# Three pieces of order in a two-layer conv and pooling trunk: reloads of x behind their units, and the products and sums of the second modulation column group

## The chip, the cores and the metric

The kernel runs on one core of one Trainium2 chip. The metric is device time in microseconds (us), the median of three runs of the same program; lower is better. A fourth execution was taken by the hardware profiler, and every time inside the kernel below is from that one.

The core's engines work side by side. PE is TensorE, which multiplies matrices; PEld is its load of weights. DVE (VectorE), ACT (ScalarE) and POOL (GpSimd) work on tiles of 128 partitions. SP (SyncE) issues DMAs, and POOL issues some too. In the trace q1 holds the DMAs that SP issues and q0 those that POOL issues.

## The reference

Sequence S = 1024, width D = 1024, feed-forward width F = 2816, two layers, all in fp32. Cut to what matters:

```
c_act = silu(c)
for i in range(2):
    mod = c_act @ ada_w[i] + ada_b[i]
    sh_m, sc_m, g_m, sh_f, sc_f, g_f = split(mod, 6)
    h = rms_norm(x) * (1 + sc_m) + sh_m
    if i == 0: y = conformer_conv(h)     # D->2D, GLU, causal taps of width 31, LayerNorm, silu, D->D
    else:      y = multiscale_pool(h)    # trailing means over 2, 4, 8, 16 minus the token, per-group linear map
    x = x + (1 + g_m) * y
    h = rms_norm(x) * (1 + sc_f) + sh_f
    x = x + (1 + g_f) * ((silu(h @ w_gate) * (h @ w_up)) @ w_down)
return rms_norm(x)
```

The six parts of `mod` are numbered j = 0 to 5 in the kernel; j = 2 is the gate of the mixer, j = 3 the shift of the feed-forward.

## The kernel before

**Products.** The tokens are two chunks, A and B, of 512. A product in fp32 is made of three products of a faster type: each operand is split into a high part and the low remainder, and high by high, high by low and low by high are added up in PSUM (`products`, L485). Most of PE's work is cut into units of 24 matmuls of 128x512 (8 slices of 128, or two halves of 4, by three products). A unit's weight comes as a raw block of 512 KB on SP's queue (tile `raw`); ACT casts it to the high part and DVE makes the low part (tiles `w`). For some weights ACT writes the negated high part, and POOL issues an adding DMA that fetches the weight a second time to make the low part.

**What sets the order.** PE's order is written out by hand: the program is a list of units, and each unit's matmuls stand where they are written. While it is written, a build-time clock adds up what PE, DVE, POOL and ACT should have spent (`clock`). After every 12 or 24 matmuls `pace` (L220) lets the waiting tasks go on: a task is a Python generator that issues its DVE, ACT and POOL instructions, and at times matmuls, in small steps. When a task yields a name, it rests: a name in `LOAD` (L55) lets it rest so many us on PE's clock, a name in `DELAY` (L66) so long behind the DVE and ACT clocks. A task marked `free` may step at every `pace`. `finish(...)` drives tasks to their end on the spot. The order on the other engines is set by a scheduler at build time; an edge (`add_manual_dep(..., edge, ...)`) tells it that an instruction stands behind another in its order, and no semaphore comes of it. Each queue then runs in that order: an SP instruction that waits holds all behind it.

**The modulation columns.** For layer 0, `ada_columns((2, 3))` (L426) computes two of the parts as columns. For each of the 8 slices of D it takes a weight block `adaw` (512 KB, SP's queue, two buffers), and four small matmuls of 32x256 add to a PSUM bank `ada`: one group of products. It yields "load" (4.0 us) ahead of each group, and when a group is done it issues the load two groups ahead. After the eighth group `columns_done` (L449) copies the bank on ACT, yields "spread" (3.0), then two small matmuls (`adac`) turn rows to columns and DVE and POOL write `mod` and the gates. It does this inside the same task, unless j is 3 and `held` is set; then it is put off to `conv_out`. In the program of before that case doesn't come up.

**The conv units and the taps.** `conv_in(*[(A, p) ...], None, *[(B, p) ...])` (L1580) writes the conv's first products for p = 6 and 7 of both chunks; at `None` it finishes the task `norm_b` that makes chunk B's `h`. Two units belong to each p: `a` and `g`. In the rows below `a_1206` is the first unit of chunk B. Behind further units of B come the taps of p = 6 and 7, on PE (`tap`). ACT adds a bias to x by `biased` (L555), which reads `gate_b`, an outcome of column group j = 2.

**The joint phase.** After the first feed-forward units of each layer, `all_joint` (L1649) runs the remaining gate and up products of both chunks jointly, in 11 joint units fp = 0 to 10 of five units of 24 matmuls each, with fewer products by combining operands and by laying partial sums aside (`rd`): the operands n and t are combinations of h, the weights s and others are combinations of four raw quarters (L1010, and by adding DMAs at L1090 and L1078). What a joint unit yields goes through tiles `r`, `t` and `g`; `g` is written to DRAM (`gd<-g`, POOL, L161) for the down products later. The tile `g` rotates, so a new `g` waits until an earlier one has been stored.

**x in DRAM.** Chunk x is spilled to DRAM ahead of this phase (`x_out`, L328: `xd<-x`) and fetched back by `x_in` (L333: `x<-xd`), four blocks of 512 KB a chunk. For chunk A the program calls `x_in(A, fp - 1)` after each of the joint units fp = 1 to 4:

```
for fp in range(NP):
    joint(l, fp)
    if 0 < fp <= KT // 2:
        unit(lambda take, m=fp - 1: x_in(A, m))
```

Nothing ties these four DMAs to PE's order. x is read again by the down products behind the joint phase (from 833 us in layer 0).

Of the kernel before, what the change touches and what calls it, by code (L numbers as in the profile page):

```python
# [19 lines left out]
KT = D // P  # L20
# [31 lines left out]

PE_TAPS = {6: 15, 7: CW}
DIAGS = 8
LOAD = {"load": 4.0, "slow": 6.0, "next": 4.0, "dots": 4.0}  # L55

ON_DVE = (1, 4)
AHEAD = 4
# [69 lines left out]
def trunk(ctx, tc, xT, c, vec, ada, adan, w1f, w1, wdg, w2, wgu, wdn, wpl, out):  # L128
# [8 lines left out]
    last_mm = [None]  # L137
    behind = [False]
    edge = mybir.DependencyInfo(mybir.DependencyClass.NoSync, mybir.DependencyReason.DATA)

    def matmul(out, lhsT, rhs, start, stop, more=False):
        n = out.shape[-1]
        clock["PE"] += n / 2400 * (1 if rhs.dtype == F32R else 4) + 0.0025
        last_mm[0] = nc.tensor.matmul(out, lhsT, rhs, start=start, stop=stop, skip_group_check=more).ins.name  # L144
# [11 lines left out]
    sync = Dma()  # L156
# [47 lines left out]
    def step(t, e):  # L204
        behind[0] = not t.urgent
        before = {k: engines[k].spent for k in "VG"}
        with tc.high_priority(offset=0 if t.urgent else -LATER):
            moved = t.step(e)
        behind[0] = False
        if V_.spent > before["V"] and getattr(t, "dots", False):  # L210
            recent.append(V_.last.ins)
            del recent[:-RECENT]
        if V_.spent > before["V"] and isinstance(t, Taps) and t.ch.i:
            beside.append(V_.last.ins)
            del beside[:-BESIDE]
        for k in "VG":
            clock[k] += (stretch[0] - 1) * (engines[k].spent - before[k])
        return moved
# [13 lines left out]
    def finish(*these):  # L232
        forced[0] = True
        for t in these:
            while not t.done:
                e = "V" if clock["V"] <= clock["G"] else "G"
                o = "VG"[e == "V"]
                if not any(step(q, e) for q in [t] + tasks) and not any(step(q, o) for q in [t] + tasks):
                    raise RuntimeError("nothing moves")
                clock["PE"] = max(clock["PE"], min(clock["V"], clock["G"]))  # L240
        forced[0] = False

    class Task:
# [6 lines left out]
        def step(self, e):  # L250
            if e != "V" or self.done or clock["PE"] < self.until and not forced[0]:
                return False
            try:
# [3 lines left out]
                if said == "wait":  # L257
                    return False
                if said in LOAD:
                    self.until = clock["PE"] + LOAD[said]  # L260
                elif said == "root":
# [12 lines left out]
    def block(tag, name, dt=F32R):  # L274

        pool, bufs = (raws, RAW_BUFS if tag == "raw" else ADA_BUFS) if tag in ("raw", "ada") else (slots, KT if tag[0] == "h" else KT // 2)
        return pool.tile([P, 2, 512], dt, tag=tag, name=nm(name), bufs=bufs)
# [15 lines left out]
    def bank(name):  # L293
        return ps.tile([P, 512], F32, tag="mm", name=nm(name))
# [27 lines left out]
    xp = [[block(f"x{ch.i}", "x", F32) for k in range(KT // 2)] for ch in chunks]  # L322
    x = [[pairs[k // 2][:, k % 2] for k in range(KT)] for pairs in xp]
    xd = [dram.tile([KT // 2, P, 2, 512], F32, name=f"xd_{i}") for i in range(2)]
# [8 lines left out]
    def x_in(ch, only=None):  # L333
        for m in range(KT // 2) if only is None else [only]:
            xp[ch.i][m] = block(f"x{ch.i}", "x", F32)
            sync.dma_start(xp[ch.i][m], xd[ch.i][m])
        x[ch.i][:] = [xp[ch.i][k // 2][:, k % 2] for k in range(KT)]
    for k in range(KT // 2):
        load_next(xp[0][k], xT[0, :, 2 * k : 2 * k + 2])
# [35 lines left out]
    def ada_load(src, queue=sync):  # L375
        w = raws.tile([P, D], F32, tag="ada", name=nm("adaw"), bufs=ADA_BUFS)
        queue.dma_start(w, src)
        return w
# [47 lines left out]
    def ada_columns(js):  # L426


        todo = [(j, k) for j in js for k in range(KT)]
        src = lambda j, k: adan[k, :, (j - 2) * D : (j - 1) * D]  # L430
        ws = [ada_load(src(*t)) for t in todo[:ADA_BUFS]]
        for i, (j, k) in enumerate(todo):
            yield "load"
            if k == 0:
                acc = bank("ada")
            w = ws.pop(0)
            for g in range(4):
                matmul(acc[32 * g : 32 * g + 32, :Q], ccols[:, k, :], w[:, g * Q : g * Q + Q], start=k == 0, stop=k == KT - 1)
            clock["PE"] -= 1.3
            if i + ADA_BUFS < len(todo):  # L440
                ws.append(ada_load(src(*todo[i + ADA_BUFS])))
            if k == KT - 1 and (j != 3 or not held[0]):
                yield from columns_done(j, acc)
            elif k == KT - 1:
                held_back.append((j, acc))

    held, held_back = [False], []

    def columns_done(j, acc):  # L449

        rows = temp(Q)
        S_.copy(rows, acc[:, :Q])
        yield "spread"
        cols = bank("adac")
        for h in range(2):
            matmul(cols[:, 4 * h : 4 * h + 4], rows[:, h * P : h * P + P], quarters, start=True, stop=True)
        m = mod[:, j * KT : (j + 1) * KT]
        V_.tensor_tensor(m.rearrange("p (q h) -> p q h", h=2), cols[:, :KT].rearrange("p (h q) -> p q h", h=2),
                         V("ada_b", j * KT, KT).rearrange("p (q h) -> p q h", h=2), op=ADD)
        ada_gains(0, j, 0, KT, G_)  # L460
        ada_done.add((0, j))
# [150 lines left out]
    def now(gen):  # L612

        while True:
            try:
                next(gen)
            except StopIteration as e:
                return e.value
# [29 lines left out]
    def unit(emit, *weights):  # L648
        units.append((weights, emit))
# [63 lines left out]
    def conv_in(*todo, fine=4):  # L713

        def emit(take):
            got = {}
            for each in todo:
                if each is None:
                    finish(T["norm_b"])
                    continue  # L720
                ch, p = each
                conv_u(ch, p)
                wts = got.setdefault(p, [])
                b = [bank("a"), bank("g")]
                for i in range(2):
                    if len(wts) == i:
                        wts.append(take())
                    for k in range(KT):
                        products(b[i], wts[i], k, st["h", ch.i][k], k == 0, k == KT - 1)
                        if k % fine == fine - 1:  # L730
                            pace()
                conv_glu(ch, p, *b, fine < 4)
                if ch.i == 0 and PE_TAPS.get(p, 0) < CW:
                    T["taps", 0, p] = Taps(A, p)
                if ch.i == 0 and p == KT - 1:
                    for q in PE_TAPS:
                        if PE_TAPS[q] < CW:
                            split_u(q)
        tiles = list(dict.fromkeys(e[1] for e in todo if e))
        unit(emit, *[w1[p, i] for p in tiles for i in range(2)])  # L740

    def split_u(p):

        u = st["u", 0, p][:, HALO - 2 : HALO - 2 + A.n]
        hi, lo = st["us", p] = pair("h0", "us")
        S_.copy(hi, u)
        either(A.n).tensor_tensor(lo, u, hi.bitcast(F32), op=SUB)
# [164 lines left out]
    def conv_out(ch, squares, then=None):  # L912

        def done(d, b):
            update(ch, d, b, gate_m, 0)
            squares.add(d)

        def emit_of(ds):
            def emit(take):
                wts = [take() for _ in ds]  # L920
                bs = [bank("y") for _ in ds]
                for k in range(KT):
                    for wt, b in zip(wts, bs):
                        products(b, wt, k, st["v", ch.i][k], k == 0, k == KT - 1)
                    if len(ds) > 1:
                        pace()
                for d, b in zip(ds, bs):
                    done(d, b)
            return emit
        for ds in [(0, 1) if ch.i else (0,), *(() if ch.i else ((1,),)), *((d,) for d in range(2, KT))]:  # L930
            unit(emit_of(ds), *[direct(w2[d]) if ch.i and d > 1 else w2[d] for d in ds])
            if then is not None and ds[0] == 0:
                unit(then)
# [530 lines left out]
    for k in range(KT):  # L1464
# [4 lines left out]
        if k > 1:  # L1469
            acc = squares[0]  # L1470
# [21 lines left out]
    for k in range(KT + 1):  # L1492
        if k < KT:
            if k:
# [4 lines left out]
                dots = [V_.last.ins]  # L1499
# [34 lines left out]
    T = {}  # L1534
# [50 lines left out]
    for p in PE_TAPS:  # L1585
        for u in pe_taps(p):
            unit(*u)
    unit(lambda take: held.__setitem__(0, True))
    unit(lambda take: finish(T["ada", 0]))
    unit(lambda take: finish(*(T["taps", 0, p] for p in range(KT) if PE_TAPS.get(p, 0) < CW)))  # L1590

    def ada_second(take):
# [7 lines left out]
    unit(lambda take: biased(A))  # L1600
    need("ln_a")
    sq_a = Squares(A, True)
    conv_out(A, sq_a, lambda take: [now(columns_done(*g)) for g in held_back])
    def scale_done(take):
        forced[0] = True
        while (0, 4) not in ada_done:
# [174 lines left out]
```

## Time and profile before

| | |
|---|---|
| three runs | 1740.39, 1738.1, 1740.81 us; median 1740.39 us |
| the profiled execution | 1738.56 us, span 1736.8 us |
| mean granted PE clock | 0.996 of full speed |
| busy, share of the span | PE 98%, DVE 75%, ACT 45%, POOL 27% |
| layer 0: modulation columns, conv units, taps | about 60 to 210 us |
| layer 0: joint phase | about 523 to 834 us |
| layer 1: start of its joint phase | about 1200 us |

In the views of the trace a row of the timeline gives start, duration, engine, line, operation, output and inputs with a count, and in brackets how long the engine had been idle before it and what ended that wait. A row of the chain of waits gives start, duration and what was running, or waited for, on the path that ended last. A row of a table of windows gives, for a stretch of time, its length, the busy time of PE, PEld, DVE, ACT and POOL with the number of instructions, then the granted PE clock, the share of the DMA engines' time that was busy, and GB/s. A DMA's time to landing is from issue to the last byte.

### The profile page before, as it was taken

The numbers are of one execution on the slowest core, as the hardware profiler recorded it, in microseconds if no ns is written. First come the engines' busy times: TensorE is split into PE (matmuls) and PEld (weight loads), VectorE is DVE, ScalarE is ACT, GpSimd is POOL, SyncE is SP. The second block draws the span as 40 slices with busy tenths as digits, with TensorE's granted clock in tenths as the row PEclk, the third lists the DMA queues.
The fourth block names the chain that finished last, engine by engine and source line by source line (L and its number), as shares of the span: only waits on it lengthen the run. The fifth ranks groups of instructions, "written<-read, shape, count | busy, mean of one in ns | idle before, by whom it ended". The sixth has DMA issues, their size and how long they took to land.

```text
span 1736.8 us, 21673 instructions
## 1 busy us (share of the span) xinstructions
PE 1701.5 (98%) x7746; PEld 1386.7 (80%) x7746; DVE 1301.8 (75%) x1878; ACT 788.3 (45%) x1080; POOL 464.2 (27%) x547
## 2 busy tenths in 40 slices
PE   7999999999998999999999999999999999999997
PEld 5777777778886888888888888888788888888887
DVE  8899898899658787887665987848677666555655
ACT  3668686876545233333223347457333333222213
POOL 2588777794001121221110301111111111000001
PEclk9999999999999999999999999999999999999999
DMA  7958987736776888887886837887777574656461
GB/s 291 300 159 236 231 232 193 209 110 198 250 227 182 269 277 244 285 247 254 312 274 214 268 113 223 241 291 202 247 219 219 167 220 141 259 206 207 166 239 56
DMA packets 111453, 385.44 MB, mean 222 GB/s; under 512 B 12145, under 2 KB 14321, under 8 KB 111346
## 3 DMA queue, kind: packets, MB, share of 16 engines
q1 hardware_dynamic: 74832, 256.11, 41.4%
q0 software_dynamic: 35424, 126.89, 29.5%
q8 instruction: 61, 1.00, 0.2%
q10 hardware_dynamic: 1090, 1.05, 0.2%
q14 instruction: 46, 0.38, 0.1%
HBM read 315.85 MB, written 63.96 MB: 219 GB/s over the span
## 4 chain that ended last, share of the span: by engine, by line
PE 87%; DVE 5%; DMA 3%; issue 3%; POOL 1%; ACT 1%; SPq 0%; DVEq 0%; POOLq 0%; ACTq 0%
PE dn L144 26%; PE a L144 22%; PE e L144 12%; PE p L144 11%; PE y L144 6%; PE g L144 3%; PE first L144 3%; PE tap L144 2%; DMA raw<-in_wgu_dram 2%; POOL pa L122 1%; PE ada L144 1%; DMA adaw<-in_adan_dram 1%; PE rstd L144 1%; DVE t L122 1%; DVE w L122 1%
## 5 line engine op out<-in xcount | busy, mean ns | idle before, releaser
L122 ACT CAST w<-raw 128x1024 fp32r<-128x1024 f32 x269 | 281.8, 1050 | 499.4 <-PE dn L144 222.6
L144 PE MATMUL dn<-g,w 128*128 128x512 f32 (+1 forms) x2184 | 484.7, 383 | 1.7 <-DVE g L122 1.0
L144 PEld LDWEIGHTS dn<-g,w 128*128 128x128 f32 x2184 | 399.7, 188 | 82.2 <-DVE g L122 1.3
L122 DVE TENSOR_TENSOR w<-raw,w 128x1024 fp32r<-128x1024 f32 x197 | 244.3, 1243 | 72.8 <-ACT w L122 71.5
L144 PE MATMUL a<-n,w 128*128 128x512 f32 x1056 | 248.0, 390 | 1.1 <-DVE n L122 0.7
L144 PE MATMUL p<-h,w 128*128 128x512 f32 x1056 | 244.1, 390 | 0.9 <-DVE h L122 0.7
L122 POOL TENSOR_TENSOR pa<-pa,pr 128x512 f32<-128x512 f32 x160 | 228.9, 1510 | 22.8 <-ACT pr L122 19.8
L144 PEld LDWEIGHTS a<-n,w 128*128 128x128 f32 x1056 | 197.7, 188 | 44.8 <-DVE n L122 2.2
L144 PEld LDWEIGHTS p<-h,w 128*128 128x128 f32 x1056 | 197.3, 188 | 43.8 <-DVE h L122 1.5
L122 DVE SCALAR_TENSOR_TENSOR x<-dn,gains,x 128x512 f32<-128x512 f32 (+1 forms) x200 | 138.5, 725 | 95.2 <-PE dn L144 95.1
L122 DVE SCALAR_TENSOR_TENSOR ca<-u,vecs,ca 128x512 f32<-128x512 f32 x245 | 169.9, 746 | 0.5
L144 PE MATMUL a<-t,w 128*128 128x512 f32 x528 | 126.5, 395 | 5.7 <-DVE w L122 2.9
L144 PE MATMUL e<-b,w 128*128 128x512 f32 x528 | 123.7, 390 | 1.6 <-DVE t L122 1.0
L144 PE MATMUL e<-t,w 128*128 128x512 f32 x528 | 123.2, 389 | 0.0
L144 PEld LDWEIGHTS a<-t,w 128*128 128x128 f32 x528 | 100.4, 191 | 28.5 <-DVE w L122 4.2
L122 ACT ACTIVATE pr<-u,vecs 128x512 f32<-128x512 f32 x160 | 108.0, 716 | 26.5 <-POOL pa L122 19.8
L144 PEld LDWEIGHTS e<-b,w 128*128 128x128 f32 x528 | 98.9, 188 | 22.9 <-DVE t L122 1.4
L1090 POOL DMA_DIRECT2D raw<-in_wgu_dram x43 | 38.1, 886 | 292.9 <-DMA raw<-in_wgu_dram 129.0
L144 PEld LDWEIGHTS e<-t,w 128*128 128x128 f32 x528 | 99.1, 188 | 20.6
L161 POOL DMA_DIRECT2D gd<-g x76 | 46.9, 619 | 192.5 <-DVE g L122 188.7
L144 PE MATMUL y<-v,w 128*128 128x512 f32 x384 | 89.2, 391 | 0.5 <-DVE v L122 0.5
L144 PEld LDWEIGHTS y<-v,w 128*128 128x128 f32 x384 | 71.5, 188 | 17.5 <-issue 1.6
(164 smaller groups left out, 1971.4 us busy)
## 6 DMA issues: line engine op xcount, KB each, us to landing
raw<-in_wgu_dram SPq DMA_DIRECT2D x132, 512.0 KB, 4.9
raw<-in_wdn_dram SPq DMA_DIRECT2D x88, 512.0 KB, 7.2
gd<-g POOLq DMA_DIRECT2D x76, 512.0 KB, 7.1
g<-gd SPq DMA_DIRECT2D x76, 512.0 KB, 5.9
adaw<-in_ada_dram POOLq DMA_DIRECT2D x48, 512.0 KB, 7.1
raw<-in_wgu_dram POOLq DMA_DIRECT2D x43, 512.0 KB, 7.1
raw<-in_w_dram SPq DMA_DIRECT2D x36, 512.0 KB, 6.6
adaw<-in_adan_dram SPq DMA_DIRECT2D x32, 512.0 KB, 5.5
```

The costliest lines, as they stand in the source:

```text
L122: self.last = self.order(getattr(self.eng, name)(out, *args, **kw))
L144: last_mm[0] = nc.tensor.matmul(out, lhsT, rhs, start=start, stop=stop, skip_group_check=more).ins.name
L161: return order(nc.gpsimd.dma_start(*a))
L1090: d = order(nc.gpsimd.dma_start(w[i], wgu[l, fp, src], accum_op=ADD))
```

## The change

It has three parts. No instruction is added or removed on any engine; the DMAs are the same and as large as before.

1. `x_in` with a single block puts an order edge on the reload: it stands behind the last matmul written so far.
2. While the units of p = 6 and 7 of chunk B are written, `dense[0]` is set, and `ada_columns` yields "dense" (0.8 us) in place of "load" (4.0 us).
3. `columns_done` for j = 2 and 3 becomes a task of its own, marked `free`, and yields "behind" (14.0 us of PE's clock) in place of "spread" (3.0). `held`, `held_back` and what `conv_out` was handed for them are gone; the unit after the taps finishes the three tasks.

```
-LOAD = {"load": 4.0, "slow": 6.0, "next": 4.0, "dots": 4.0}
+LOAD = {"load": 4.0, "dense": 0.8, "behind": 14.0, "slow": 6.0, "next": 4.0, "dots": 4.0}
...
-            sync.dma_start(xp[ch.i][m], xd[ch.i][m])
+            d = sync.dma_start(xp[ch.i][m], xd[ch.i][m])
+            if only is not None:
+                tc.add_manual_dep(d.ins, last_mm[0], edge, reason="behind the unit")
...
-            yield "load"
+            yield "load" if not dense[0] else "dense"
...
-            if k == KT - 1 and (j != 3 or not held[0]):
+            if k == KT - 1 and j < 4:
+                T["ada", j] = Task(columns_done(j, acc), False, 0)
+                T["ada", j].free = True
+            elif k == KT - 1:
                 yield from columns_done(j, acc)
-            elif k == KT - 1:
-                held_back.append((j, acc))
-
-    held, held_back = [False], []
+
+    dense = [False]
...
-        yield "spread"
+        yield "behind" if j < 4 else "spread"
...
                 if each is None:
                     finish(T["norm_b"])
+                    dense[0] = True
                     continue
...
+            dense[0] = False
...
-    unit(lambda take: held.__setitem__(0, True))
-    unit(lambda take: finish(T["ada", 0]))
+    unit(lambda take: finish(T["ada", 0], T["ada", 2], T["ada", 3]))
...
-    conv_out(A, sq_a, lambda take: [now(columns_done(*g)) for g in held_back])
+    conv_out(A, sq_a)
```

**PE, units of chunk B in the conv.** `a` and `g` are the conv's products (a row is three matmuls of one slice), `ada` a group of the second column group (j = 3), `adac` the turning to columns of j = 2. Before, one group stands between two units, and the turning ahead of `g_1207`:

```order
L144 MATMUL a_1206<-h_774,w_678 128x512 x3
L144 MATMUL adac_1236<-quarters,t_1176 128x4 x2
L144 MATMUL g_1207<-h_767,w_823 128x512 x3
L144 MATMUL g_1207<-h_768,w_823 128x512 x3
L144 MATMUL g_1207<-h_769,w_823 128x512 x3
L144 MATMUL g_1207<-h_770,w_823 128x512 x3
L144 MATMUL g_1207<-h_771,w_823 128x512 x3
L144 MATMUL g_1207<-h_772,w_823 128x512 x3
L144 MATMUL g_1207<-h_773,w_823 128x512 x3
L144 MATMUL g_1207<-h_774,w_823 128x512 x3
L144 MATMUL ada_1283<-adaw_1119,ccols 32x256 x4
```

And at the same place in the changed kernel:

```order
L144 MATMUL a_1206<-h_774,w_678 128x512 x3
L144 MATMUL ada_1236<-adaw_1119,ccols 32x256 x4
L144 MATMUL g_1207<-h_767,w_823 128x512 x3
L144 MATMUL g_1207<-h_768,w_823 128x512 x3
L144 MATMUL g_1207<-h_769,w_823 128x512 x3
L144 MATMUL g_1207<-h_770,w_823 128x512 x3
L144 MATMUL ada_1236<-adaw_1174,ccols 32x256 x4
L144 MATMUL g_1207<-h_771,w_823 128x512 x3
L144 MATMUL g_1207<-h_772,w_823 128x512 x3
L144 MATMUL g_1207<-h_773,w_823 128x512 x3
L144 MATMUL g_1207<-h_774,w_823 128x512 x3
L144 MATMUL ada_1236<-adaw_1241,ccols 32x256 x4
```

The first group moved from behind `g_1207` to ahead of it, and a group now stands after every 12 matmuls. This goes on to the eighth group in the middle of the third pair's `a`; before, the eighth stood among the taps. The turning of j = 2 moved to the middle of the next unit `a`, and that of j = 3 from among the taps to ahead of them.

**SP, at the same time.** `raw<-in_wdg` are the taps' weights; the rows are all of SP's between the loads of the conv's units and those of the units behind the taps. Before:

```order
L471 DMA raw_1473<-in_wdg_dram 128x1024
L154 DMA adaw_1288<-in_adan_dram 128x1024
L154 DMA adaw_1341<-in_adan_dram 128x1024
L471 DMA raw_1530<-in_wdg_dram 128x1024
L154 DMA adaw_1391<-in_adan_dram 128x1024
L471 DMA raw_1539<-in_wdg_dram 128x1024
L154 DMA adaw_1461<-in_adan_dram 128x1024
L471 DMA raw_1643<-in_wdg_dram 128x1024
L471 DMA raw_1650<-in_wdg_dram 128x1024
L154 DMA adaw_1514<-in_adan_dram 128x1024
L471 DMA raw_1699<-in_wdg_dram 128x1024
L154 DMA adaw_1580<-in_adan_dram 128x1024
```

And now:

```order
L154 DMA adaw_1241<-in_adan_dram 128x1024
L474 DMA raw_1503<-in_wdg_dram 128x1024
L154 DMA adaw_1270<-in_adan_dram 128x1024
L154 DMA adaw_1299<-in_adan_dram 128x1024
L474 DMA raw_1551<-in_wdg_dram 128x1024
L154 DMA adaw_1339<-in_adan_dram 128x1024
L154 DMA adaw_1364<-in_adan_dram 128x1024
L474 DMA raw_1560<-in_wdg_dram 128x1024
L154 DMA adaw_1392<-in_adan_dram 128x1024
L474 DMA raw_1653<-in_wdg_dram 128x1024
L474 DMA raw_1660<-in_wdg_dram 128x1024
L474 DMA raw_1703<-in_wdg_dram 128x1024
```

The six loads of the second column group moved ahead of the last three tap weights; two of them stand side by side twice. On ACT the bias operations `x<-x,gate_b`, which stood ahead of two casts of conv weights, now stand behind them.

**SP, start of the joint phase of layer 0.** `raw<-in_wgu` are quarters of joint weights (`raw_4807` the last of fp = 1, `raw_5044` the first of fp = 2), `r<-rd` parts of sums that were laid aside, `x<-xd` the reloads. Before:

```order
L1010 DMA raw_4807<-in_wgu_dram 128x1024
L154 DMA x_5208<-xd_87 128x1024
L154 DMA x_5410<-xd_87 128x1024
L154 DMA x_5612<-xd_87 128x1024
L154 DMA x_5818<-xd_87 128x1024
L154 DMA r_820_5210<-rd_2_179 128x512
L1010 DMA raw_5044<-in_wgu_dram 128x1024
```

And now, `raw_5244` to `raw_5250` being those of fp = 3:

```order
L1010 DMA raw_4807<-in_wgu_dram 128x1024
L154 DMA r_820_5210<-rd_2_179 128x512
L1010 DMA raw_5044<-in_wgu_dram 128x1024
L1010 DMA raw_5046<-in_wgu_dram 128x1024
L1010 DMA raw_5048<-in_wgu_dram 128x1024
L1010 DMA raw_5050<-in_wgu_dram 128x1024
L154 DMA r_821_5211<-rd_2_179 128x512
L1010 DMA raw_5244<-in_wgu_dram 128x1024
L1010 DMA raw_5246<-in_wgu_dram 128x1024
L154 DMA x_5208<-xd_87 128x1024
L1010 DMA raw_5248<-in_wgu_dram 128x1024
```

The first reload moved behind two quarters of fp = 3; the other three stand in the same way among the quarters of fp = 4, 5 and 6. In layer 1 it is alike: four reloads among the quarters of fp = 1 before, one each among those of fp = 3 to 6 now.

## The prediction

> **What bounds the kernel now.** I read the page's busy times first, then the windows, to find where TensorE isn't busy or not at full clock; then PE's timeline there, the chain of waits and the DMA view.
>
> ```profile
> PE 1701.5 (98%) x7746; PEld 1386.7 (80%) x7746; DVE 1301.8 (75%) x1878; ACT 788.3 (45%) x1080; POOL 464.2 (27%) x547
> 550.00:555.00 5.00, 4.24 (x18) 2.88 (x16) 0.00 (x0) 0.06 (x1) 0.00 (x0) 1.00 0.99 382
> 555.00:560.00 5.00, 0.93 (x3) 0.49 (x4) 4.41 (x6) 2.64 (x4) 0.55 (x1) 0.78 1.04 314
> 560.00:565.00 5.00, 5.00 (x13) 3.90 (x14) 4.13 (x5) 4.26 (x5) 0.53 (x1) 0.54 0.34 134
> 600.00:763.00 163.00, 163.00 (x721) 134.95 (x720) 134.13 (x180) 52.36 (x66) 34.44 (x57) 1.00 0.86 264
> ```
>
> PE is the bound: 98% of 1736.8 us, so 35.3 us idle in all, and inside the joint phase none between 600 and 763. Work taken off another engine is worth nothing unless PE waits for it. What can be won is idle time of PE and time at a lower clock; both stand together at the start of layer 0's joint phase, 555 to 565, where the granted clock is 0.78 and 0.54 beside 1.00 around it.
>
> ```profile
> 543.53 10.71 PE L144 MATMUL a<-n,w 128*128 128x512 f32 x41 [0.73 <-DVE n L122]
> 557.08 0.73 PE L144 MATMUL a<-t,w 128*128 128x512 f32 x2 [2.84 <-ACT w L122]
> 559.80 7.51 PE L144 MATMUL a<-t,w 128*128 128x512 f32 x22 [1.99 <-DVE w L122]
> 567.16 5.60 PE L144 MATMUL e<-t,w 128*128 128x512 f32 x24
> 572.60 5.60 PE L144 MATMUL a<-n,w 128*128 128x512 f32 x24
> ```
>
> A unit of 24 matmuls takes 572.60 - 567.16 = 5.44 us, 0.227 a matmul. The unit `a<-t` waits 2.84 + 1.99 = 4.83 us, and its last 22 matmuls take 7.51 us where 22 x 0.227 = 4.99 would do: 2.5 us lost to the clock. Together 7.3 us. Why it waits:
>
> ```profile
> 545.88 8.98 DMA gd<-g
> ...
> 554.94 0.63 ACT g L122
> ...
> 558.62 1.14 DVE w L122
> ...
> 559.80 7.51 PE a L144 x22
> ```
>
> ACT's cast of the next `g` stands ahead of the cast of the weight that PE needs, and waits for the tile `g` to be stored: 8.98 us from issue to landing. From there to PE's restart it is 559.80 - 554.86 = 4.94 us of ACT and DVE work.
>
> **Part 1, layer 0: the reloads go out of the way of that store.**
>
> ```profile
> 545.17 6.01 SPq L154 DMA_DIRECT2D x<-xd  x4
> 545.33 0.87 POOL L1285 DMA_DIRECT2D n<-af  x1 [1.63 <-issue]
> 545.88 1.41 POOL L161 DMA_DIRECT2D gd<-g  x2
> 547.86 0.88 POOL L1090 DMA_DIRECT2D raw<-in_wgu_dram  x1 [0.57 <-DVE raw L122]
> 564.67 1.31 SPq L1010 DMA_DIRECT2D raw<-in_wgu_dram  x3
> q0 software_dynamic: 326, 0.58, 64.8%
> q1 hardware_dynamic: 162, 0.60, 43.7%
> ...
> q1 hardware_dynamic: 269, 0.99, 52.3%
> q0 software_dynamic: 251, 0.92, 47.0%
> DMA to landing us min/median/max: 2.9/6.8/13.9
> ```
>
> Four reloads (2 MB) are issued between 545.2 and 551.2, the two stores of `g` at 545.9 to 547.3, in the midst of them. The q rows are the DMA view of 545 to 550 and of 550 to 555: in these ten us q1, which holds nothing but the reloads, takes 43.7% and 52.3% of the DMA engines' time. The last row is the landing of all stores of `g` in the run: 2.9 at best, 6.8 at the median, 13.9 at worst; this one, at 8.98, is a slow one. Both queues are busy all through, so without q1 the work of q0 in these ten us (64.8% and 47.0%, 5.6 us of all engines) could be done in about 5.6. I take 5.5 us for the landing, 3.5 earlier. The bounds are the best landing, 2.9 (6.1 earlier), and the median, 6.8 (2.2 earlier); no gain at all is a rival below, and a loss I exclude, because nothing else is put into this window: in SP's order the next weights' loads waited for their buffers until 564.67 before.
>
> Then PE's idle shrinks from 4.83 to about 1.3 us. A clock of 0.78 over 555 to 560 is half of full speed for 0.22 x 5 / 0.5 = 2.2 us, so from about 558 on, after idle of 2.84 and 1.99 us with 0.73 of work between; after 1.3 it should not come, which is 2.5 us more. Sum: 3.5 + 2.5 = **6.0 us** (2.2 if the clock still drops, 4.83 + 2.5 = 7.3 at most). A rule of the Trainium skill ("TensorE: Matmul & The Clock Gate", What's actually happening) bears on this: the clock halves after an idle window of about 3.4 us, and is either full or half. The trace agrees with the drop after 4.83 us of idle; by the rule even an idle of 2.6 would be too short, and the sum at the lower bound would be 2.2 + 2.5 = 4.7 rather than 2.2. The same skill ("DMA: Bandwidth & Descriptors", Queues, rings and completion order) says that each DMA engine takes turns between the queues that have work; the trace's two shares near one half agree, and by that rule the store would land in about half of 8.98, for a sum of 4.83 - 0.3 + 2.5 = 7.0.
>
> What is late next? The unit behind needs a weight whose adding load was issued at 547.86, in the same window behind the stores; it too gets the reloads' share. I count nothing for it, up to 2 us of loss if it doesn't land sooner.
>
> The reloads come back one to a joint unit. A joint unit is 5 units, 27.2 us, and 512 KB are a quarter of those 2 MB, which took 96% of five us of all engines: 4.8 / 4 = 1.2 us, a load of 4% on top of the 0.86 above. What hides it:
>
> ```profile
> 579.58 1.21 DVE L122 TENSOR_TENSOR w<-s,w 128x1024 fp32r<-128x1024 f32 x1
> 588.92 3.34 PE L144 MATMUL a<-t,w 128*128 128x512 f32 x14
> ```
>
> The first weight of fp = 2 is ready at 580.79 and used at 588.92, 8.1 us ahead. A reload in SP's queue delays the load behind it by a few us at most, and x is read again only by the down products behind the joint phase. I count 0; with the cover gone, 4 x 1.2 = 5 us.
>
> **Part 1, layer 1.** The same code, but little is lost here:
>
> ```profile
> 1206.45 6.91 SPq L154 DMA_DIRECT2D x<-xd  x3
> 1206.99 5.32 PE L144 MATMUL a<-t,w 128*128 128x512 f32 x22 [0.33 <-DVE w L122]
> 1230.07 5.29 PE L144 MATMUL a<-t,w 128*128 128x512 f32 x22 [0.58 <-DVE w L122]
> 1249.92 3.01 PE L144 MATMUL e<-b,w 128*128 128x512 f32 x12 [0.97 <-DVE t L122]
> 1213.46 9.24 DMA raw<-in_wgu_dram
> ```
>
> The raw block that leads to the second of these waits was issued behind three reloads and took 9.24 us. Its wait of 0.58 should go and the third shrink; the first ends when the reloads have only begun. I take **0.9 us** of the 1.88, bounds 0 and 1.9.
>
> **Parts 2 and 3: the second column group.** The counts are the same, so its PE time is too; only waits can change.
>
> ```profile
> 118.51 0.64 PE L144 MATMUL ada<-adaw,ccols 128*32 128x256 f32 x8
> 119.08 5.74 PE L144 MATMUL a<-h,w 128*128 128x512 f32 x24
> 169.18 0.64 PE L144 MATMUL ada<-adaw,ccols 128*32 128x256 f32 x8 [1.03 <-DMA adaw<-in_adan_dram]
> DMA to landing us min/median/max: 3.3/4.1/6.7
> ...
> DMA to landing us min/median/max: 11.7/12.3/12.8
> 120.00:130.00 10.00, 10.00 (x48) 8.34 (x47) 9.93 (x16) 7.64 (x13) 9.69 (x11) 1.00 0.23 69
> 130.00:145.00 15.00, 15.00 (x82) 10.67 (x81) 15.00 (x25) 15.00 (x25) 9.54 (x9) 1.00 0.59 168
> 145.00:160.00 15.00, 15.00 (x77) 11.26 (x76) 13.36 (x21) 14.23 (x19) 12.23 (x12) 1.00 0.97 249
> ```
>
> The two landing rows are the `adaw` loads issued from 95 to 156 (eight) and from 156 to 165 (two). A group costs 119.08 - 118.51 = 0.57 us. The wait of 1.03 at 169.18, whose load travelled among the tap weights with the DMA engines full, goes: the last group now stands before 150. Against it, groups follow each other after 12 matmuls: 2.72 + 0.57, and some 0.2 for the switches, 3.5 us instead of 6.2. With two buffers a load has two such spaces less one group, 2 x 3.5 - 0.57 = 6.4 us, from issue to use. Landings of 3.3 to 6.7 just fit that. I put some waits at 0.4 us in all, and the bias operations that ACT now does later at nothing, since the conv casts they made late stand ahead of them now. So 1.03 - 0.4, and of this half may be lost again in later waits of the conv for DVE: **0.3 us**, bounds below (-18) and 1.4.
>
> **The sum.** 6.0 + 0.9 + 0.3 = 7.2 us off the profiled execution's 1738.56, 1731.4. The median of the runs is 1740.39, 1.83 above that execution; I forecast **1733 us** on that footing. Since PE has no idle time in the joint phases to take a gain back, what is won at their start reaches the end.
>
> **The rivals.**
>
> *The store is slow by itself (16%).* Ahead of it POOL issued adding DMAs for `n`, the last at 545.33, and two stores and an adding load share q0. If q0 sets its landing, it falls by no more than to the median, 2.2 us, PE still idles 2.6, and the clock drops all the same. Gain 2.2 + 0.9 + 0.3 = 3.4, 1737 us. Against it: q1's half of the engines' time. This lies on the edge of no change.
>
> *The dense loads come late (13%), the one that ends slower.* PE runs in order, so a late block stops it. If a load takes 12.3 us, as the two of 156 to 165 did, a group comes every (12.3 + 0.57) / 2 = 6.4 us instead of 3.5, and the six loads issued inside the stretch cost 6 x 2.9 = 17 us: 1740.39 - 7 + 17 = 1750 us. It cancels part 1 when a wait is 7.2 / 6 = 1.2 a group, at landings of 2 x 4.7 - 0.57 = 8.8 us. The stretch now lies at 125 to 150, where the share was 0.23 and 0.59; loads twice as dense add about 0.2. Only its end touches 0.97. So I give 7% to slower than before, 5% to a draw, 1% to a gain.
>
> *The change doesn't part the reloads (3%).* An edge orders without a wait. But SP's queue is in order, and each reload now stands behind quarters that wait for buffers. It would leave 1740.
>
> **How the numbers follow.** The forecast, a gain of 4 to 10 us, has 68%. A measurement of this kernel can tell about 0.2%, 3.5 us. Faster by more: 68, the lower third of the first rival's 16 (6), and 1: 75%. Within it: 10 + 5 + 3 = 18%. Slower: 7%. The range goes from 1727.5, where the upper bounds nearly meet (7.3 + 1.9 + 1.4 = 10.6, and runs 2 us apart), up to 1739, which takes in the first rival and small waits of the second; about 15% is left out.
>
> **What would show it.** Right: the store of `g` near 546 lands in 5 to 6 us, `a<-t` waits under 2 us, the clock is 1.0 from 555 to 565, four reloads stand one to a joint unit, no wait at the last `ada` group. Wrong: the same landing without reloads beside it; waits of 1 us and more at `ada` groups between 125 and 150; a wait of PE in fp = 3 to 6 behind a reload.

## The result, and the profile after

The changed kernel takes 1734.31 us at the median of 7 runs (1732.17 to 1736.31), the kernel before 1739.37 us of 7 (1736.47 to 1741.88). The ratio is 0.9972, with a 95% interval of 0.9961 to 0.9984: 5 us faster. 1733 was forecast, from 1727.5 to 1739. The time is right, yet of its terms one has the wrong sign and one effect of 2.5 us was not foreseen; that the sum came so near is in part luck, as the errors below show.

The profiled execution of the changed kernel has a span of 1733.9 us, 2.9 less than that of before. Marks in PE's timeline show where the two part. These rows of the changed kernel's timeline are the marks, each the start of the same unit as in before: the first `a` of the conv, the last unit ahead of the joint phase's stall, the unit behind the stall, the first down product behind the joint phase, and a unit at the start of layer 1's joint phase.

```profile
68.83 5.74 PE L144 MATMUL a<-h,w 128*128 128x512 f32 x24 [0.75 <-ACT t L122]
539.03 5.74 PE L144 MATMUL e<-b,w 128*128 128x512 f32 x24 [0.61 <-DVE r L122]
564.12 5.60 PE L144 MATMUL e<-t,w 128*128 128x512 f32 x24
833.21 17.16 PE L144 MATMUL dn<-g,w 128*128 128x512 f32 x75
1200.62 5.60 PE L144 MATMUL e<-t,w 128*128 128x512 f32 x24
```

In the kernel before the same units start here (the second and third stand in the prediction, at 535.14 and 567.16):

```profile
67.37 5.73 PE L144 MATMUL a<-h,w 128*128 128x512 f32 x24 [0.76 <-ACT t L122]
833.72 16.48 PE L144 MATMUL dn<-g,w 128*128 128x512 f32 x72
1200.60 5.60 PE L144 MATMUL e<-t,w 128*128 128x512 f32 x24
```

| stretch | before | after | difference |
|---|---|---|---|
| up to the first `a` of the conv | 67.37 | 68.83 | +1.5 |
| conv, taps, first feed-forward units | 467.77 | 470.20 | +2.4 |
| stall at the joint phase's start | 32.02 | 25.09 | -6.9 |
| the rest of layer 0's joint phase | 266.56 | 269.09 | +2.5 |
| down products, pooling, up to 1200 | 366.88 | 367.41 | +0.5 |
| from there to the span's end | 536.20 | 533.28 | -2.9 |

The first row lies ahead of the units that the change reorders, and the same stretch takes 66.7 to 69.4 us in the other kernels' profiles; it is left out of account. The rest comes to -4.4, near the 5.1 between the medians.

**The stall at the joint phase's start.** PE's timeline and the chain of waits of the changed kernel:

```profile
557.73 0.61 PE L144 MATMUL a<-t,w 128*128 128x512 f32 x2
558.99 5.29 PE L144 MATMUL a<-t,w 128*128 128x512 f32 x22 [0.65 <-DVE w L122]
```

```profile
549.82 4.23 DMA gd<-g
554.12 0.63 ACT g L122
...
557.81 1.14 DVE w L122
558.99 5.29 PE a L144 x22
```

The store of `g` lands in 4.23 us instead of 8.98. From its landing to PE's restart it is 558.99 - 554.05 = 4.94 us, as before. Of the idle of 4.83 us 0.65 is left, and the last 22 matmuls take 5.29 instead of 7.51. The windows show the clock:

```profile
555.00:560.00 5.00, 4.35 (x19) 3.30 (x18) 3.94 (x5) 1.98 (x3) 0.55 (x1) 1.00 0.85 209
560.00:565.00 5.00, 5.00 (x23) 4.13 (x22) 4.68 (x6) 4.18 (x6) 0.53 (x1) 1.00 0.14 44
600.00:763.00 163.00, 162.10 (x716) 133.83 (x715) 132.44 (x179) 51.36 (x66) 34.35 (x57) 1.00 0.87 272
```

**Two new waits behind it.** The last window has 0.90 us idle where there was none. PE's timeline further on, and DVE's at the same places:

```profile
575.00 2.88 PE L144 MATMUL e<-b,w 128*128 128x512 f32 x12
578.64 3.01 PE L144 MATMUL e<-b,w 128*128 128x512 f32 x12 [0.76 <-DVE t L122]
...
604.53 5.69 PE L144 MATMUL e<-b,w 128*128 128x512 f32 x24 [0.90 <-DVE t L122]
```

```profile
576.76 1.23 DVE L122 TENSOR_TENSOR s<-raw,raw 128x1024 f32<-128x1024 f32 x1 [7.61 <-DMA raw<-in_wgu_dram]
577.90 0.69 DVE L122 TENSOR_TENSOR t<-e,r 128x512 f32<-128x512 f32 x1
...
602.55 1.23 DVE L122 TENSOR_TENSOR raw<-raw,s 128x1024 f32<-128x1024 f32 x1 [2.70 <-DMA raw<-in_wgu_dram]
603.70 1.28 DVE L122 TENSOR_TENSOR t<-e,r 128x512 f32<-128x512 f32 x2
```

Both times `t`, which empties the bank that PE needs next, stands on DVE behind a sum of raw quarters that waits for its load: 7.61 and 2.70 us. DVE was free for `t` long before. At the second place the order was the same before the change, only PE came later. At the first the order itself is new: DVE's rows in program order before the change, at the end of fp = 1,

```order
L122 TENSOR_TENSOR t_5073<-e_5059,r_790_5010 128x512
L122 TENSOR_TENSOR t_5087<-e_5060,r_791_5011 128x512
L122 TENSOR_TENSOR s_800_5054<-raw_5044,raw_5046 128x1024
```

and behind it:

```order
L122 TENSOR_TENSOR t_5073<-e_5059,r_790_5010 128x512
L122 TENSOR_TENSOR g_5003<-t_5000,g_5003 128x512
L122 TENSOR_TENSOR s_800_5054<-raw_5044,raw_5046 128x1024
L122 TENSOR_TENSOR t_5087<-e_5060,r_791_5011 128x512
```

With the reloads out of SP's queue the scheduler placed the sum of fp = 2 ahead of the second `t` of fp = 1.

**The dense column products.** PE's timeline of the changed kernel in the conv, the chain of waits there, and a window:

```profile
141.19 3.02 PE L144 MATMUL g<-h,w 128*128 128x512 f32 x12
146.10 0.64 PE L144 MATMUL ada<-adaw,ccols 128*32 128x256 f32 x8 [1.88 <-DMA adaw<-in_adan_dram]
146.67 4.61 PE L144 MATMUL g<-h,w 128*128 128x512 f32 x12
137.81 8.24 DMA adaw<-in_adan_dram
145.00:150.00 5.00, 3.90 (x16) 2.82 (x17) 5.00 (x8) 5.00 (x10) 3.36 (x4) 0.68 1.04 309
```

One load of the six takes 8.24 us to land with the DMA engines full, PE waits 1.88 us for it, and then the 12 matmuls behind it take 4.61 us instead of 3.02, at a granted clock of 0.68 in that window. 1.88 + 1.59, less the wait of 1.03 that the kernel before had in the taps, is 2.4: the second row of the table.

**Layer 1.** The second and third of the three waits are gone:

```profile
1228.86 5.62 PE L144 MATMUL a<-t,w 128*128 128x512 f32 x24
1234.31 5.60 PE L144 MATMUL e<-t,w 128*128 128x512 f32 x24
...
1245.19 5.60 PE L144 MATMUL e<-b,w 128*128 128x512 f32 x24
1250.63 5.60 PE L144 MATMUL a<-n,w 128*128 128x512 f32 x24
```

### The profile page after: what moved, and what is told of

Its sections match the earlier page's. It is cut to its first block, busy times and chain, and to the rows that moved or that the text cites. A ratio compares the mean times of both kernels' runs of the same rounds, so it can differ in the third digit from the quotient of the medians.

```text
span 1733.9 us, 21656 instructions
## 1 busy us (share of the span) xinstructions
PE 1700.8 (98%) x7746; PEld 1387.0 (80%) x7746; DVE 1306.2 (75%) x1878; ACT 788.2 (45%) x1080; POOL 462.8 (27%) x547
## 4 chain that ended last, share of the span: by engine, by line
PE 86%; DVE 6%; DMA 2%; issue 2%; ACT 1%; POOL 1%; DVEq 0%; ACTq 0%; SPq 0%; POOLq 0%
PE dn L144 26%; PE a L144 22%; PE e L144 12%; PE p L144 10%; PE y L144 5%; PE g L144 3%; PE first L144 3%; PE tap L144 2%; DMA raw<-in_wgu_dram 1%; DVE t L122 1%; POOL pa L122 1%; PE ada L144 1%; DVE w L122 1%; PE rstd L144 1%; PE var L144 1%
```

## The experiments

Ratios are to the kernel before, run beside each on the same chip, with a 95% interval; kernels are compared with one another by their ratios.

### The change taken apart

**Reloads alone.** The kernel before with `x_in`'s edge and nothing else:

```
+            d = sync.dma_start(xp[ch.i][m], xd[ch.i][m])
+            if only is not None:
+                tc.add_manual_dep(d.ins, last_mm[0], edge, reason="behind the unit")
```

> Only the reloads' edge (both layers), modulation columns as before. Theory: the three parts add up by place. In the two profiles the start of layer 0's joint phase gains 6.9 us, two new waits of PE for DVE behind it give back 2.4, layer 1 gains 2.4, and the conv phase loses 2.4 to the late column load. So without the columns' part the kernel is faster than before by about 7 us (ratio 0.996), and PE shows no wait at an ada group but the one of about 1 us among the taps. Rival: the columns' part costs nothing once other waits take it up; then the gain is that of the whole change, 5 us (0.9972).

0.9970 (0.9958 to 0.9982), 1733.55 us: 5.6 us faster than before's 1739.14. The store lands in 4.23 us again, the two waits of PE for `t` are there (0.75 and 0.94 us), and no group of the second column group waits. The ratio lies between theory and rival, nearer the rival, and the interval holds both: in the times, leaving the columns out is worth 0.0002 against the changed kernel's 0.9972, where the profiles' 2.4 us would be 0.0014.

**Columns alone.** The changed kernel without that edge:

> Only the dense column products and their sums as own tasks; the reloads as before. Theory: 2 to 3 us slower than before (ratio 1.0012 to 1.0018): one wait of about 1.9 us at an ada group and some 3 us at half clock behind it (1.5 lost), less the wait of 1.0 that is gone from the taps; the start of the joint phase shows the same idle of 4.8 us as before. Rival: no difference beyond 0.05%, because later waits for DVE in the conv take the loss up.

1.0016 (1.0007 to 1.0024), 1741.74 us: slower, as the theory had it. PE's timeline shows the late load, the half clock behind it, and the stall at the joint phase's start:

```profile
136.75 0.75 PE L144 MATMUL ada<-adaw,ccols 128*32 128x256 f32 x8 [1.58 <-DMA adaw<-in_adan_dram]
137.43 4.45 PE L144 MATMUL a<-h,w 128*128 128x512 f32 x12
...
557.67 0.73 PE L144 MATMUL a<-t,w 128*128 128x512 f32 x2 [1.08 <-ACT w L122]
560.40 6.87 PE L144 MATMUL a<-t,w 128*128 128x512 f32 x22 [1.99 <-DVE w L122]
567.10 5.60 PE L144 MATMUL e<-t,w 128*128 128x512 f32 x24
```

The stall is smaller than the 4.83 us expected. Here the store of `g` landed in 7.35 us, and the stretch that took 32.02 us in the profile of before takes 567.10 - 537.24 = 29.86. So the profile of before had caught a costly execution. What the reloads' move saves there is 4.8 us against this execution and 6.9 against that. With the reloads moved, the same stretch takes 25.05 to 25.25 us in all eleven profiles.

**One layer each.** The reloads' edge in layer 0 only, and in layer 1 only (`x_in(A, m, l == 0)` and `l == 1`, the columns as before):

> Only the reloads' edge, and only in layer 0. Theory: 4 to 4.5 us faster than before (ratio 0.9975), 6.9 at the joint phase's start less the two new waits; the store of g lands in under 5 us beside no reload. Rival: the store lands late by itself and another of the changes shortened it; then no gain here.

0.9976 (0.9967 to 0.9984), as the theory had it. The store's rival falls: with nothing changed but the reloads, the two stores land at a median of 4.7 us, as in every other kernel whose reloads are moved (4.6 to 4.7), and of 9.9, 8.2 and 7.8 in the three profiles where they are not.

> Only the reloads' edge, and only in layer 1. Theory: 2.4 us faster than before (ratio 0.9986), the waits near 1230 and 1250 gone, that near 1207 unchanged. Rival: the third wait hangs on work of DVE and stays; then 0.9 us (0.9995).

0.9982 (0.9974 to 0.9991): at least what the theory had. Both later waits are gone and the first is there at 0.32 us, so the third hung on the reloads too. In the profile of before the chain of waits runs from the second to the third. In the profile the stretch from the unit `e<-t` near 1200 to the last root near the end falls from 527.9 us to 525.5. Its layer 0 is that of before, and shows a third size of the stall: 565.46 - 536.05 = 29.41 us.

```profile
536.05 5.73 PE L144 MATMUL e<-b,w 128*128 128x512 f32 x24 [0.63 <-DVE r L122]
...
565.46 5.60 PE L144 MATMUL e<-t,w 128*128 128x512 f32 x24
```

**Dense or not.** The changed kernel with `"dense": 4.0`, one group at each unit, the sums still tasks of their own:

> The changed kernel with "dense" at 4.0 us, so that one group stands at each unit again; the sums stay tasks of their own, the reloads stay tied. Theory: the loss in the conv comes of the spacing alone; no wait of 1.9 us and no half clock near 146, so 2.5 us faster than the changed kernel and about 7 faster than before (ratio 0.996). Rival: the loss comes of the later sums or of ACT's moved bias operations; then it stays, and the ratio is 0.997.

0.9964 (0.9952 to 0.9975), no wait and no half clock at these groups. The same kernel again, beside the last three:

> One column group at each unit, sums as own tasks, reloads tied, once more beside the three others. It gives what the two edges on DVE are compared with: ratio 0.9964 as before, within 0.001.

0.9960 (0.9947 to 0.9972). The intervals overlap with the changed kernel's; the profiles decide. From the conv's first `a` to the last unit ahead of the stall it is 469.3 to 470.5 us in the three with dense groups (the changed kernel, the columns alone, and the changed kernel with one edge on DVE, below), and 466.7 to 468.5 in the other eleven. So the loss is the spacing's, not that of the sums or of ACT's moved bias operations. With the spacing loosened at every second group only,

```
-            yield "load" if not dense[0] else "dense"
+            yield "load" if not dense[0] or k % 2 else "dense"
```

> The changed kernel with "dense" only at every second group of the second column group; groups stand 12 or 24 (once 36) matmuls apart. Theory: a load's time from issue to use is what decides; the closest pair of spacings is now 12 and 24 matmuls, 3.5 + 6.2 - 0.6 = 9 us for a load, above the 8.2 that the late one took, so no wait over 0.5 us at these groups, and 2 us faster than the changed kernel (0.996 to 0.9965). Rival: the loads land later the closer they come, and PE still waits; then 0.997.

0.9960 (0.9948 to 0.9973), no wait at the second column group, and equal to one group a unit. That fits the theory that the two buffers' time for a load decides, but the rival has a part in it: the slowest `adaw` load issued from 118 to 170 us took 8.2 to 8.7 us in the three dense kernels, and 6.3 to 6.5 in the four whose sums are own tasks and whose groups stand further apart. How much is less time and how much later landing was not parted.

**Reloads together, but later.** All four behind joint unit fp = 4:

```
-            if 0 < fp <= KT // 2:
-                unit(lambda take, m=fp - 1: x_in(A, m))
+            if fp == KT // 2:
+                unit(lambda take: [x_in(A, m) for m in range(KT // 2)])
```

> All four reloads of a layer tied together behind joint unit fp = 4, columns as before: away from the store, but not parted. Theory: what matters is that they don't travel beside the store; the joint phase starts as in the changed kernel (idle under 1 us, no half clock), and the bunch of 2 MB costs PE less than 1 us later, so the time is that of the reloads' edge alone, about 7 us faster than before (0.996). Rival: parting them matters too; the weights of the joint unit behind the bunch come 4 to 5 us late, and PE waits there 1 us or more.

0.9974 (0.9965 to 0.9983), not told apart from the reloads alone at 0.9970. The stall at the start is as small (555.46, 0.69 us), and the bunch, issued at 662.6, is followed by one wait of 0.17 us. But the load right behind the bunch, issued at 667.12, took 15.00 us, where the slowest of these loads from 655 to 735 us takes 8.7 with the reloads alone. And a wait of 1.91 us stands at 740, for `t` behind a sum whose load was issued at 728.82; it is the one shown below under the clock. In the chain of waits that ends there, the load of 15.00 us stands too. The joint phase took 274.02 us in this profile, one of the slower runs (1738.66), against 268.99 with the reloads alone. What matters first, then, is that the reloads don't travel beside the store; whether parting them also matters stays open, and this profile speaks for the rival.

### The two new waits

**The sum of fp = 2 behind the second t of fp = 1**, by an edge on DVE, as it stood before:

```
+            if fp == 2 and e is V_:
+                ...
+                    tc.add_manual_dep(V_.last.ins, st["t1_last"], edge, reason="behind the last t")
```

> The changed kernel with one more edge: the sum s of raw weight quarters of fp = 2 stands on DVE behind the second t of fp = 1, as it did in the kernel before. Theory: the new wait of 0.76 us near 578 comes of that swap, since s waits 7.6 us for its load and holds t, which PE waits for; with the edge it is gone, and the time falls by up to 1.2 us. Rival: the same DMA chain (quarters of fp = 3) ends PE's lead anyway; then the wait near 604 grows by as much (from 0.9 to about 2 us), and the time is the same.

> The reloads' edge and the edge for s, columns as before. Theory: the best of both, 7 us from the reloads and up to 1.2 more: ratio 0.9953 to 0.996. Rival: PE's lead is ended by the loads of fp = 3 in any case; ratio 0.996 as with the reloads alone.

On the changed kernel: 0.9983 (0.9975 to 0.9992); on the reloads alone: 0.9966 (0.9954 to 0.9978). The wait near 578 is gone in both, but the one near 602 grew from 0.90 to 1.22 us and from 0.94 to 1.96, as the rival said, and neither is faster for it. In the second the clock halves on top:

```profile
602.71 7.33 PE L144 MATMUL e<-b,w 128*128 128x512 f32 x24 [1.96 <-DVE t L122]
```

That the first came out slower than the changed kernel (its runs spread from 1732.2 to 1738.8) is not explained; its profile is one of the faster runs.

**Both sums behind t.** The edge above, and the sum into the fourth quarter of fp = 3 (`raw<-raw,s`) behind the second `t` of fp = 2:

```
     def s4():
-            either(D).tensor_tensor(w[1], w[1], w[4], op=ADD)
+            e = either(D)
+            e.tensor_tensor(w[1], w[1], w[4], op=ADD)
+            behind_t(e)
```

> The reloads' edge, columns as before, and on DVE two sums of raw quarters behind the t that PE waits for: s of fp = 2 behind the second t of fp = 1, and the sum into the fourth quarter of fp = 3 behind the second t of fp = 2. In the profile of the changed kernel, of the reloads alone and with only the first of these edges PE waits 0.9, 0.9 and 1.2 to 2.0 us near 602 for t, which stands behind that second sum, which waits for its load. Theory: the lead won at the joint phase's start is given back there by DVE's order, not by the load itself; with both edges no wait near 575 or 602, and the time from unit e<-t near 561 to the one near 1200 falls from 636 to about 633.5 us, so 2 us faster than with the reloads alone (ratio 0.9955). Rival: the lead runs out on the loads; then a wait for a weight w stands there instead, and the ratio stays 0.997.

> The same two edges on the changed kernel with one column group at each unit (the sums of the columns as own tasks, reloads tied). Theory: both gains add, ratio 0.9950 to 0.9955, the fastest of all. Rival as before: 0.9964, as without the two edges.

0.9951 (0.9938 to 0.9965) at 1731.42 us, and 0.9951 (0.9939 to 0.9964) at 1732.05. These are the fastest two; beside them, on the same chip, the kernel without the two edges took 1733.18. Intervals overlap, so the gain of some 1 to 2 us rests on the profiles too: both waits are gone (the first kernel has one of 0.41 us for `r` at 592.64 instead), here in the second of the two kernels,

```profile
572.90 5.60 PE L144 MATMUL e<-b,w 128*128 128x512 f32 x24
578.59 5.81 PE L144 MATMUL a<-n,w 128*128 128x512 f32 x24
...
600.76 5.60 PE L144 MATMUL e<-b,w 128*128 128x512 f32 x24
```

and its joint phase, from `e<-t` at 562.02 to the first down product at 829.92, takes 267.90 us, against 269.09 in the changed kernel and 266.56 before. The first of them takes 826.68 - 559.42 = 267.26. Without the two edges it is 268.99 (reloads alone) and 269.14 (one group a unit). So 1.2 to 1.7 of the 2.5 us were held up by the order on DVE and not by the loads; what holds the rest was not traced. Nor does all of it reach the next layer: from `e<-t` to the one near 1200 these two take 635.55 and 634.95 us, against 635.91 and 636.33 without the edges, where the theory had 633.5. In the first, the down products wait 1.50 us for `x` at 962.92 (0.24 with the reloads alone). The separate column tasks add nothing that shows.

## Why the prediction was right or wrong

**What bounds the kernel, and the stall: right.** PE's idle and half clock at 555 to 565 were the place, the store of `g` beside the reloads the cause (4.23 against 8.98 us), and the half clock went with the idle. 6.0 us were forecast and 6.9 measured between the two profiles. 5.5 us for the landing was too long; the likely reason, which was not tested, is that dividing the two queues' time still charged the store with the adding loads that share q0. But the size was also flattered by the one profile: against the two other executions whose reloads were not moved, the gain is 4.8 and 4.3 us. The rival of a store slow by itself is refuted by the kernel that changes layer 0 alone.

**"What is won at their start reaches the end": wrong.** This is the step that failed. The argument was that PE has no idle time in the joint phase to take a gain back. It had none because it came late enough: a PE that is not held up at the start meets work that had just been ready. The margin that was looked at, 8.1 us, was that of the weight, whereas the binding one was that of `t`. In the profile of before, DVE's timeline has it here:

```profile
603.35 1.28 DVE L122 TENSOR_TENSOR t<-e,r 128x512 f32<-128x512 f32 x2
```

The row is two operations of 0.68 us, and the unit waits for the first alone: in the changed kernel PE starts at 604.53, before the second is done at 604.98. So before, `t` was done at 604.03 for a unit that started at 605.24, 1.2 us ahead. 2.5 us were given back, and in the two kernels with two sums moved on DVE the joint phase is 1.2 to 1.8 us shorter.

**The reloads among the joint units at no cost: right as far as shown.** The first reload is issued at 584.83, behind the first new wait; and the wait near 604 hangs on a load issued at 594.19, whose landing of 8.34 us can be set beside 8.7 for the same load in the profile of before. Both new waits also stand in the kernel whose reloads all come later (0.88 and 1.53 us), so no reload causes them.

**Layer 1: the right mechanism, mis-sized.** 0.9 us was taken, 2.2 is what the two waits cost: from `a<-t` to `e<-t` 6.32 became 5.45, and from `e<-b` to the next `a<-n` 6.81 became 5.44. A wait costs about 0.3 to 0.4 us more than the idle in its row (0.58 cost 0.87, 0.97 cost 1.37), since a matmul's row lasts 0.39 us where matmuls follow each other at 0.227: part of the gap is counted as busy. And the third wait fell entirely.

**Parts 2 and 3: the wrong sign.** Waits were put at 0.4 us in all; one alone cost 3.5, by the very rule of the slower rival: 6.4 us from issue to use, a landing of 8.24. Five of the six loads came in time, so that rival's price was out of reach, but its mechanism is real: alone, this part makes the kernel 2.6 us slower. What the working missed is the half clock behind a wait of 1.9 us, which nearly doubled it. The share of the DMA engines at that place, taken from the kernel before as 0.59 plus 0.2, was 0.95 from 130 to 145 us and 1.04 behind it. And the wait of 1.03 us, which the forecast counted as won, is not a fixed price: of the seven profiles with the columns as before it stands in two (1.03 and 1.01).

7.2 us were forecast and 5.1 measured. The errors cancelled in part, which is luck: 0.9 more at the stall and 1.3 more in layer 1 than forecast, against 2.7 less in the conv and 2.5 less in the joint phase. The rows of 0.5 us in the table were not followed up.

## What to carry to other kernels

Ask of every gain at a stall how far ahead the next things are ready, engine by engine, and include small results such as a bank being emptied: an order on a queue that was harmless while PE came late is the next bound. A load that nothing needs for a long time should not start beside a store on which the next work waits; an order edge suffices to move it. And packing loads closer than buffers times spacing allows turns a late load (one or two of six in each dense profile here) into a stop of PE, which runs its units in order.

## What was not expected of the hardware

The clock fell to 0.50 after much shorter idle time than the 4.83 us of the stall: after waits of 1.58, 1.88, 1.91 and 1.96 us, each for 3.41 us, at a cost of 1.4 to 1.7 us (12 matmuls in 4.45 or 4.61 for 3.02, 24 in 7.33 for 5.60). So the prediction's remark that idle of 2.6 us would be too short does not hold here, and at the stall itself the clock was down from 557.80 on, before the second of its two waits. One of these waits, in the kernel with the reloads together:

```profile
740.43 7.33 PE L144 MATMUL e<-b,w 128*128 128x512 f32 x24 [1.91 <-DVE t L122]
```

Yet a longer wait, 2.29 us for the same late load in the kernel with the first edge on DVE, left the clock at 1.00:

```profile
146.05 0.64 PE L144 MATMUL ada<-adaw,ccols 128*32 128x256 f32 x8 [2.29 <-DMA adaw<-in_adan_dram]
146.62 3.04 PE L144 MATMUL g<-h,w 128*128 128x512 f32 x12
```

One of 1.61 us at a group of the first column group (at 86.81, in the kernel with the reloads together) didn't cost it either. The traces show what decides: where the wait falls in time. In each of the fourteen profiles all changes of the granted clock, from the start on, lie on one grid of steps of 3.413 us, which starts elsewhere in each execution. Three windows of the columns alone, then one of the kernel with the first edge on DVE:

```profile
133.74:137.15 3.41, 1.83 (x17) 1.32 (x15) 3.41 (x6) 3.34 (x6) 3.41 (x4) 1.00 1.03 314
137.15:140.57 3.42, 3.42 (x15) 2.48 (x8) 3.42 (x3) 0.37 (x1) 3.42 (x5) 0.50 1.04 249
560.40:563.82 3.42, 3.42 (x8) 2.74 (x9) 1.79 (x3) 1.73 (x2) 0.53 (x1) 0.50 0.88 343
142.27:145.68 3.41, 1.49 (x7) 0.90 (x5) 3.41 (x4) 3.02 (x6) 3.41 (x5) 1.00 1.03 318
```

From 137.15 to 560.40 it is 423.25 us, 124 steps. In the kernel before, half clock lasted two steps, 557.80 to 564.63, and that is part of why its stall was the longest of the three. The clock falls behind a step in which PE does too little. As an estimate, each matmul of 128x512 is counted as the last 0.227 us of its row, and smaller ones in proportion to their size. Then beyond the first 60 us PE works at most 40% of the step ahead of each of the 21 falls from full to half clock, and at least 41% of every step at full clock that no fall follows. The wait of 2.29 us is cut by a mark of the grid at 145.68, that of 1.61 us by one at 85.75, so PE still works 44% and 50% of the step with the longer part. The border is read off these executions alone; no run was made to test it.
